# The SSD decay matrices move from the attention stage to the gate projections

## The chip, the cores and the metric

The kernel runs on one core of a Trainium2 chip. The metric is the device time of one execution in microseconds; several executions are taken and their median is given. In the profile PE is the matmul engine and PEld its weight load, DVE the vector engine, ACT the engine for activation functions, POOL the general one, and SP the engine whose queue issues every DMA of this kernel.

## The reference

Two layers run over 1024 latent and 256 context tokens of width 1024. Each layer normalizes its tokens, projects them once, and feeds three branches: a state-space scan in two directions (SSD), grouped-query attention, and a conformer branch. The outputs are concatenated and projected back. The part of the SSD that the change touches, for chunks of 128 tokens:

```python
seg = cum[:, :, :, None] - cum[:, :, None, :]
mask = jnp.tril(jnp.ones((l, l), dtype=bool))[None, None, :, :, None, None]
lmat = jnp.exp(jnp.where(mask, seg, -jnp.inf))
cb = jnp.einsum('bclgn,bcsgn->bclsg', Cc, Bc)
y_diag = jnp.einsum('bclsg,bclsgr,bcsgrp->bclgrp', cb, lmat, xdt)
...
u = ua * jax.nn.sigmoid(ub)
u = jax.nn.silu(layernorm(dwconv(u, conv_w, conv_b), ln_g, ln_b))
u = u @ pw_w + pw_b
return u * jax.nn.silu(gate)
```

The last four lines are the conformer branch. The product of `cb` and `lmat` is the masked decay matrix, called E here: for each chunk, direction and group of six heads one tile of 128 x 768 numbers.

## The kernel before, in words

Tokens come in ten tiles of 128 (eight latent, two context). Large products run as three fp32r matmuls, since each operand is split into a high and a low part: `mm3` (L210) issues high times high, low times high, high times low, all through `mm` (L193). Transposes go through `tr` (L196), activations through `act` (L199), vector operations through `ts` (L203, L205) and `stt` (L208), and the power of -1/2 through `rs_pow` (L269, L271 on POOL). The order of instructions on each engine comes from a scheduler that follows priorities: `at(us)` sets the priority of what follows, and lower goes first. It also follows the pools: a pool has a fixed number of buffers for each name, they are handed out in the order in which the program asks for them, and who asks later waits for who asked earlier. PSUM has four pools: `pm` with four buffers ("m"), `pt` with two ("t"), `pv_` with one ("v") and `px` with one ("x").

`phase_b` (L434) makes the projections. After q, k and v it runs 17 weight blocks, `block(i)` (L623), each due 26 us after the one before. `wblock` (L349) loads the block's weights, copies them to `wth` on ACT and takes `wtl`, the rest, by a subtraction on POOL (L359). Blocks 0 to 8 give the inputs of the SSD and the conformer branch; their convolutions run on DVE, `conv_x` writes B and C transposed to DRAM (`bT_d`, `cT_d`), and `cac` holds the four convolved tiles of the conformer branch. Blocks 9 to 16 give the gates: `gate` (L590) takes a tanh on ACT, a product on DVE and stores the result (`gz_d`, `gc_d`, `ga_d`).

Beside blocks 11 to 16 runs the conformer branch's end, `cm_tail` (L656). For each tile of tokens it transposes `cac` into a "t" buffer, takes the mean and variance on DVE, normalizes (`xn`, one buffer), transposes back into the "x" buffer, scales and shifts (`lv`, L205), takes a tanh and a product, and splits the result into `uh` (ACT) and `ul` (POOL, L689), with one buffer for each of the two. For a group of tiles, (0,4), (4,4) and (8,2), in layer 1 the first two, the pointwise GEMM follows: for each of four blocks of features twelve matmuls into the "v" buffer, an eviction that multiplies by the gate (`gcs`, loaded from `gc_d`), and a store to `yc_d`.

Attention comes next, and the SSD's scan runs beside it. `attn_prep` (L841) prepares keys and queries: `kprep` (L849) loads `k_t` (L856, one buffer) in three parts, splits it on ACT and DVE (L860) and transposes it through the "v" buffer. `attn` (L904) issues the score products (`k_a`, `q_a`), takes maxima on DVE (`a_sm`, L935), exponentials on ACT (`a_p`), sums on DVE and POOL (`a_ac`, L974) and the scaled output (`a_a`, L981). `ssd` (L710) takes the chunks 25 us apart. For each chunk it loads B and C, multiplies them into the "x" buffer, masks the product on DVE (`s_cm`, L772), and for each direction and group loads the cumulative log decays as a broadcast (`s_cb`, L785), subtracts on POOL (L788), applies a relu and an exponential on ACT, and multiplies by the masked product on POOL (L791).

Of the kernel before, what the change touches and what calls it, by code (L numbers as in the profile page):

```python
# [9 lines left out]
F32R = mybir.dt.float32r  # L10
# [150 lines left out]
def build(tc, a, out, depth=DEPTH, dump=None):  # L161
# [4 lines left out]
    def at(us):  # L166
        tc.cur_priority = int(us * 100)

    def pool(st, name, bufs=1, **k):
        return st.enter_context(tc.tile_pool(name=name, bufs=bufs, **k))  # L170
# [3 lines left out]
    def mk(p, shape, tag, dt=F32, bufs=None):  # L174
        uid[0] += 1
        k = {} if bufs is None else {"bufs": bufs}
        return p.tile(shape, dt, tag=tag, name=f"{tag}_{uid[0]}", **k)
# [8 lines left out]
    def dr(shape, name, dt=F32):  # L186
        t = dp.tile(shape, dt, tag=name, name=name)
        if dump is not None:
            dump[name] = t
        return t  # L190

    def mm(o, l, r, start, stop):
        P.matmul(o, l, r, start=start, stop=stop)  # L193
# [4 lines left out]
    def act(o, i, f, **k):  # L198
        S.activation(o, i, f, **k)  # L199
# [58 lines left out]
    bT_d = dr([2, 128, T], "bT_d")  # L258
    cT_d = dr([2, 128, T], "cT_d")
    cum_d = dr([NT * 24, 128], "cum_d")  # L260
    gz_d = dr([6, 128, T], "gz_d")
    ga_d = [dr([128, T], f"ga_d{j}") for j in range(6)]
    gc_d = [dr([128, T], f"gc_d{j}") for j in range(4)]
# [170 lines left out]
    def phase_b(l, nh, b0, pp):  # L434
# [122 lines left out]
        def conv_x(j, t0):  # L557
            xp = xps[j]
            at(t0)
            o = mk(xp_p, [128, 1282], "xcv", bufs=2)  # L560
            w = sw[:, 5 * j:5 * j + 5]
            ts(V, o, xp[:, 0:1282], w[:, 0:1], ALU.mult, sw[:, 50 + j:51 + j], ALU.add)
            for k in range(1, 5):
                at(t0 + 2 * k)
                stt(o, xp[:, k:k + 1282], w[:, k:k + 1], o, ALU.mult, ALU.add)
            at(t0 + 10)
            th = mk(up_p, [128, 1282], "th")
            act(th, o, AF.Tanh)
            stt(o, th, 1.0, o, ALU.add, ALU.mult)
            if j >= 6:  # L570
                d = bT_d[j - 6] if j < 8 else cT_d[j - 8]
                Y.dma_start(out=d[:, 0:1024], in_=o[:, 0:1024])
                Y.dma_start(out=d[:, 1024:1280], in_=o[:, 1026:1282])
            if j < 8:
                at(t0 + XLAG)
                sg = mk(gp, [128, NT, 128], "xsg")
                for ta in (0, 4, 8):
                    n = min(4, NT - ta)
                    ps = mk(*((pt, [128, 4, 128], "t") if ta == 4 else (px, [128, 4, 128], "x")))
                    for t in range(ta, ta + n):  # L580
                        c0 = t * 128 + (2 if t >= 8 else 0)
                        tr(ps[:, t - ta, :], o[:, c0:c0 + 128], idf)
                    act(sg[:, ta:ta + n, :], ps[:, 0:n, :], AF.Copy)
                if j < 6:
                    d = xt_d[:, :, 128 * j:128 * j + 128]
                else:
                    d = bt_d[:, :, 128 * (j - 6):128 * (j - 6) + 128]
                Y.dma_start(out=d.rearrange("t p f -> p t f"), in_=sg)
# [64 lines left out]
        for i in range(9, 14):  # L653
            block(i)

        def cm_tail(c0):  # L656
            at(c0 - 10)
            pwh, pwl = wblock(tlp, wt, a["pww"][l], "pw", 1)
            hc = mk(tlp, [128, 16], "hc")
            ts(V, hc[:, 0:8], colc[l][:, CO["lng"][0]:CO["lng"][0] + 8], 0.5, ALU.mult)  # L660
            groups = [(0, 4), (4, 4)] + ([] if last else [(8, 2)])
            for tb, tn in groups:
                uh = mk(tlp, [128, 4, 512], "uh", F32R)
                ul = mk(tlp, [128, 4, 512], "ul", F32R)
                for t in range(tb, tb + tn):
                    at(c0 + 4 * t)
                    c1 = t * 128 + (15 if t >= 8 else 0)
                    ps = mk(pt, [128, 4, 128], "t")
                    for j in range(4):
                        tr(ps[:, j, :], cac[j][:, c1:c1 + 128], idf)  # L670
                    bs = mk(tlp, [128, 12], "bs", bufs=2)
                    V.bn_stats(bs[:, 0:6], ps.rearrange("p j t -> p (j t)"))
                    V.bn_aggr(bs[:, 6:8], bs[:, 0:6])
                    rs_pow(bs[:, 9:10], bs[:, 7:8], 1.0, bs[:, 8:9], 1)
                    xn = mk(gp, [128, 512], "xn", bufs=1)
                    ts(V, xn, ps.rearrange("p j t -> p (j t)"), bs[:, 6:7], ALU.subtract, bs[:, 9:10], ALU.mult)
                    ps2 = mk(px, [128, 4, 128], "x")
                    for j in range(4):
                        tr(ps2[:, j, :], xn[:, 128 * j:128 * j + 128], idf)
                    th = mk(tlp, [128, 4, 128], "lth", bufs=1)  # L680
                    v2 = mk(tlp, [128, 4, 128], "lv2", bufs=1)
                    for j in range(4):
                        g, b = hc[:, j:j + 1], hc[:, 4 + j:5 + j]
                        ts(V, v2[:, j], ps2[:, j], g, ALU.mult, b, ALU.add)
                    act(th, v2, AF.Tanh)
                    stt(v2, th, 1.0, v2, ALU.add, ALU.mult)
                    o = (t - tb) * 128
                    act(uh[:, :, o:o + 128], v2, AF.Copy)
                    G.tensor_tensor(ul[:, :, o:o + 128], v2, uh[:, :, o:o + 128].bitcast(F32), ALU.subtract)  # L689
                n = tn * 128  # L690
                at(c0 + 4 * (tb + tn))
                for f in range(4):
                    gcs = mk(gp, [128, 512], "gcs")
                    Y.dma_start(out=gcs[:, 0:n], in_=gc_d[f][:, tb * 128:tb * 128 + n])
                    ps = mk(pv_, [128, 512], "v")
                    pwx, ux = (pwh, pwl), (uh, ul)
                    mm3(ps[:, 0:n], lambda x, k: pwx[x][:, k, 128 * f:128 * f + 128],
                        lambda x, k: ux[x][:, k, 0:n], 4)
                    stt(gcs[:, 0:n], ps[:, 0:n], cc(l, "pwb", f), gcs[:, 0:n], ALU.add, ALU.mult)
                    ts(V, gcs[:, 0:n], gcs[:, 0:n], 0.5, ALU.mult)  # L700
                    Y.dma_start(out=yc_d[f][:, tb * 128:tb * 128 + n], in_=gcs[:, 0:n])
# [8 lines left out]
    def ssd(l, sp, c0, sv):  # L710
# [15 lines left out]
        def bc(x, n=NH, w=HD):  # L726
            return x.unsqueeze(2).to_broadcast([128, n, w])
# [27 lines left out]
        for c in [8, 9] + list(range(8)):  # L755
# [1 line left out]
            t0 += SSD_PACE  # L757
            xt, bt = load(c)
            if c < 8 or not last:
                bT = mk(sp, [128, 2, 128], "s_bT", bufs=2)  # L760
                cT = mk(sp, [128, 2, 128], "s_cT", bufs=2)
                tk = slice(128 * c, 128 * c + 128)
                Y.dma_start(out=bT, in_=bT_d[:, :, tk].rearrange("g p t -> p g t"))
                Y.dma_start(out=cT, in_=cT_d[:, :, tk].rearrange("g p t -> p g t"))
                gz = mk(sp, [128, 6, 128], "s_gz", bufs=1)
                Y.dma_start(out=gz, in_=gz_d[:, :, tk].rearrange("g p t -> p g t"))
                ps = mk(px, [128, 512], "x")
                for g in range(2):
                    mm(ps[:, 128 * g:128 * g + 128], bT[:, g, :], cT[:, g, :], True, True)
                cm = mk(sp, [128, 2, 2, 128], "s_cm", bufs=1)  # L770
                for d, m in enumerate((um, lm)):
                    V.tensor_tensor(cm[:, d], ps[:, 0:256].rearrange("p (g t) -> p g t", g=2),  # L772
                                    m.unsqueeze(1).to_broadcast([128, 2, 128]), ALU.mult)
                xd = []
                for d in range(2):
                    t = mk(sp, [128, 768], f"s_xd{d}", bufs=1)
# [2 lines left out]
                E = {}  # L779
                for g in range(2):  # L780
                    for d in range(2):
                        h0 = 12 * d + 6 * g
                        cb = mk(sp, [128, 6, 128], "s_cb", bufs=2)
                        src = cum_d[24 * c + h0:24 * c + h0 + 6, :].rearrange("h t -> (h t)")
                        Y.dma_start(out=cb.rearrange("p h t -> p (h t)"),  # L785
                                    in_=src.unsqueeze(0).to_broadcast([128, 768]))
                        e = mk(sp, [128, 6, 128], "s_e", bufs=4)
                        G.tensor_tensor(e, cb, bc(cum[:, c, h0:h0 + 6], 6, 128), ALU.subtract)  # L788
                        act(e, e, AF.Relu, scale=-1.0)
                        act(e, e, AF.Exp, scale=-1.0)  # L790
                        G.tensor_tensor(e, e, cm[:, d, g].unsqueeze(1).to_broadcast([128, 6, 128]), ALU.mult)  # L791
                        E[d, g] = e
                yo = mk(sp, [128, 768], "s_yo", bufs=1)
                G.tensor_tensor(hv(yo), hv(xt), bc(rc(l, "d")), ALU.mult)
# [412 lines left out]
```

## Time and profile before

| | |
|---|---|
| runs, us | 2926.68, 2923.34, 2924.92 |
| median, us | 2924.92 |
| profiled execution, us | 2925.86 |
| its span, us | 2924.0 |
| mean granted PE clock | 0.976 of full |
| DMA traffic | 314.44 MB, 108 GB/s over the span |

The span runs from the first to the last instruction that the profiler shows; the profiled execution's own time is 1.9 us longer. Busy time counts an engine from the start to the end of its instructions; matmuls overlap, so their mean duration is longer than the distance from one start to the next. The stages follow each other within each layer: the gate projections of layer 0 lie at 534 to 799 us and its attention at 806 to 1360, those of layer 1 at 2017 to 2226 and 2236 to 2730. In a row of a group the count stands behind an x, then the busy time in us and the mean duration of one in ns, then the engine's idle time before them and what ended it.

### The profile page before, as it was taken

To read this page: it belongs to the slowest core of one execution; us is meant where nothing else is said; L and a number is where in the kernel's file an instruction comes from. 1 tells how busy PE (TensorE), PEld (TensorE's weight loads), DVE (VectorE), ACT (ScalarE), POOL (GpSimd) and SP (SyncE) were. 2 spreads that over 40 slices of the span, in tenths; PEclk is the share of its full clock that TensorE was granted. 3 is DMA by queue.
4 is the path that set the end of the run, shared out by engine and by line. 5 is a ranking of instruction groups with operands and counts; after the bars stand their busy time and mean duration, and the time that the engine had idled before them with its cause. 6 is when DMAs were issued, how large, how long until landed. Compare 5 with 4: busy or idle time off the path is not lost. (4 is left out here: it accounts for less than half of the span.)

```text
span 2924.0 us, 41060 instructions
## 1 busy us (share of the span) xinstructions
PE 2775.7 (95%) x15708; PEld 2058.5 (70%) x15708; DVE 2167.2 (74%) x2987; ACT 1068.0 (37%) x1801; POOL 1167.3 (40%) x832
## 2 busy tenths in 40 slices
PE   5999998999999999899999999999998999999998
PEld 3888876888855555565787998877886565555676
DVE  4576899973288889887545577999834889898744
ACT  4212221222245555454335322222223455644532
POOL 2244122232166767662112353122322676775111
PEclk8999998999999999999999999999999999999999
DMA  6541111223342323223745322113335232321654
GB/s 237 191 160 66 56 55 62 92 92 112 101 144 84 102 68 104 67 76 99 213 153 161 122 77 68 56 55 98 111 118 168 74 98 77 95 64 43 185 154 144
DMA packets 284035, 314.44 MB, mean 108 GB/s; under 512 B 27606, under 2 KB 219190, under 8 KB 282814
## 3 DMA queue, kind: packets, MB, share of 16 engines
q1 hardware_dynamic: 283838, 311.82, 33.5%
q8 instruction: 123, 2.02, 0.3%
q14 instruction: 74, 0.61, 0.1%
HBM read 236.25 MB, written 75.50 MB: 107 GB/s over the span
## 5 line engine op out<-in xcount | busy, mean ns | idle before, releaser
L193 PE MATMUL m<-hh,wth 128*128 128x512 f32 (+1 forms) x1440 | 534.9, 371 | 0.1
L193 PE MATMUL m<-hl,wth 128*128 128x512 f32 (+1 forms) x1440 | 533.4, 370 | 0.0
L193 PE MATMUL m<-hh,wtl 128*128 128x512 f32 (+1 forms) x1440 | 532.7, 370 | 0.0
L199 ACT ACTIVATE a_p<-m 128x512 f32<-128x512 f32 x492 | 289.0, 595 | 374.0 <-PE m L193 370.6
L208 DVE SCALAR_TENSOR_TENSOR cac<-up,cmw,cac 128x1295 f32<-128x1295 f32 (+1 forms) x240 | 385.4, 1627 | 2.0
L935 DVE TENSOR_REDUCE a_sm<-m 128x1 f32<-128x512 f32 (+1 forms) x600 | 332.5, 582 | 46.9 <-PE m L193 45.0
L359 POOL TENSOR_TENSOR wtl<-wr,wth 128x1024 fp32r<-128x1024 f32 x68 | 200.3, 2945 | 406.6 <-ACT wth L199 406.6
L193 PE MATMUL t<-a_p,vs 128*64 128x256 f32 x1968 | 324.0, 405 | 0.7 <-DVE a_rc L1010 0.3
L193 PEld LDWEIGHTS m<-hh,wth 128*128 128x128 f32 x1440 | 274.0, 190 | 48.0 <-ACT th L199 0.5
L193 PEld LDWEIGHTS m<-hh,wtl 128*128 128x128 f32 x1440 | 273.5, 190 | 48.3
L193 PEld LDWEIGHTS m<-hl,wth 128*128 128x128 f32 x1440 | 273.8, 190 | 47.4
L193 PE MATMUL m<-q_a,k_a 128*128 128x512 f32 (+1 forms) x656 | 259.7, 406 | 6.1 <-DVE a_sm L935 4.6
L193 PE MATMUL m<-k_a,q_a 128*128 128x512 f32 (+1 forms) x600 | 247.0, 437 | 13.6 <-DVE a_sm L935 9.8
L193 PE MATMUL m<-woh,yh 128*128 128x512 f32 x576 | 225.8, 395 | 8.2 <-issue 3.3
L193 PE MATMUL m<-woh,yl 128*128 128x512 f32 x576 | 228.8, 398 | 4.4 <-DVE yl L1099 4.3
L193 PE MATMUL m<-wol,yh 128*128 128x512 f32 x576 | 226.5, 394 | 0.0
L193 PE MATMUL m<-q_b,k_b 65*128 65x512 f32 (+1 forms) x656 | 218.8, 344 | 0.0
L193 PEld LDWEIGHTS m<-q_a,k_a 128*128 128x128 f32 x656 | 125.9, 192 | 107.1 <-issue 52.0
L193 PEld LDWEIGHTS t<-a_p,vs 128*64 128x64 f32 x1968 | 104.3, 136 | 133.9 <-issue 95.3
L193 PEld LDWEIGHTS m<-k_a,q_a 128*128 128x128 f32 x600 | 113.5, 195 | 113.3 <-issue 45.2
L199 ACT ACTIVATE wth<-wr 128x1024 fp32r<-128x1024 f32 (+1 forms) x84 | 89.3, 1064 | 256.3 <-DMA wr<-in_wfm 134.5
L193 PE MATMUL m<-wth,hh 128*128 128x256 f32 (+1 forms) x608 | 173.7, 288 | 0.6 <-DVE c_qn L474 0.5
(239 smaller groups left out, 5604.4 us busy)
## 6 DMA issues: line engine op xcount, KB each, us to landing
wr<-in_wfm SPq DMA_DIRECT2D x68, 512.0 KB, 3.6
s_cb<-cum_d SPq DMA_DIRECT2D x72, 384.0 KB, 3.7
ada_w<-in_adaw SPq DMA_DIRECT2D x32, 512.0 KB, 4.2
wor<-in_wout SPq DMA_DIRECT2D x64, 256.0 KB, 3.1
s_x<-xt_d SPq DMA_DIRECT2D x38, 384.0 KB, 3.0
yf<-ys_d SPq DMA_DIRECT2D x36, 384.0 KB, 4.0
yf<-ya_d SPq DMA_DIRECT2D x36, 384.0 KB, 4.2
yf<-yc_d SPq DMA_DIRECT2D x36, 256.0 KB, 2.9
```

The lines of the kernel that those rows point to most:

```text
L193: P.matmul(o, l, r, start=start, stop=stop)
L199: S.activation(o, i, f, **k)
L208: V.scalar_tensor_tensor(o, i, s, i1, op0, op1)
L359: (e or G).tensor_tensor(lo[:, s], raw, hi[:, s].bitcast(F32), ALU.subtract)
L935: V.tensor_reduce(sm[:, 2 * x + t, j:j + 1], ps[:, 0:kn], axis=AX.X, op=ALU.max)
```

## The change

A new function, `decays`, makes the four matrices E of a chunk and stores them to a new DRAM tensor, one for each chunk. It is called for all chunks behind `block(13)` and ahead of `cm_tail` in the program, 18 us apart from 8 us after block 9's due time. In `ssd` the code that made E is gone, and four loads stand in its place. To make room, the conformer tail works on pairs of tiles, five in layer 0 and four in layer 1: `uh`, `ul` and `gcs` are half as wide, `gcs` has two buffers, and a helper tile, `xsg`, moves to another pool. In `decays`, the product of B and C uses the "x" buffer, e_b, e_c and the masked product e_m have one buffer each, and E (`e_e`) has three.

```diff
+    e_d = [dr([4, 128, 768], f"e_d{c}") for c in range(NT)]
...
-                sg = mk(gp, [128, NT, 128], "xsg")
+                sg = mk(xp_p, [128, NT, 128], "xsg")
...
         for i in range(9, 14):
             block(i)
+        def decays(c, t0):
+            cum = sv[1]
+            tk = slice(128 * c, 128 * c + 128)
+            at(t0)
+            bT = mk(ep, [128, 2, 128], "e_b")
+            cT = mk(ep, [128, 2, 128], "e_c")
+            Y.dma_start(out=bT, in_=bT_d[:, :, tk].rearrange("g p t -> p g t"))
+            Y.dma_start(out=cT, in_=cT_d[:, :, tk].rearrange("g p t -> p g t"))
+            at(t0 + 2)
+            ps = mk(px, [128, 512], "x")
+            for g in range(2):
+                mm(ps[:, 128 * g:128 * g + 128], bT[:, g, :], cT[:, g, :], True, True)
+            cm = mk(ep, [128, 2, 2, 128], "e_m")
+            for d, m in enumerate((um, lm)):
+                V.tensor_tensor(cm[:, d], ps[:, 0:256].rearrange("p (g t) -> p g t", g=2),
+                                m.unsqueeze(1).to_broadcast([128, 2, 128]), ALU.mult)
+            for d in range(2):
+                for g in range(2):
+                    h0 = 12 * d + 6 * g
+                    at(t0 + 4 * (2 * d + g))
+                    e = mk(ep, [128, 6, 128], "e_e", bufs=3)
+                    src = cum_d[24 * c + h0:24 * c + h0 + 6, :].rearrange("h t -> (h t)")
+                    Y.dma_start(out=e.rearrange("p h t -> p (h t)"), in_=src.unsqueeze(0).to_broadcast([128, 768]))
+                    G.tensor_tensor(e, e, bc(cum[:, c, h0:h0 + 6], 6, 128), ALU.subtract)
+                    act(e, e, AF.Relu, scale=-1.0)
+                    act(e, e, AF.Exp, scale=-1.0)
+                    G.tensor_tensor(e, e, cm[:, d, g].unsqueeze(1).to_broadcast([128, 6, 128]), ALU.mult)
+                    Y.dma_start(out=e_d[c][2 * d + g], in_=e.rearrange("p h t -> p (h t)"))
+
+        ep = pool(s3, f"ep{l}")
+        for i, c in enumerate(range(8) if last else [8, 9] + list(range(8))):
+            decays(c, g0 + 8 + 18 * i)
...
-            groups = [(0, 4), (4, 4)] + ([] if last else [(8, 2)])
+            groups = [(b, 2) for b in range(0, 8 if last else NT, 2)]
             for tb, tn in groups:
-                uh = mk(tlp, [128, 4, 512], "uh", F32R)
-                ul = mk(tlp, [128, 4, 512], "ul", F32R)
+                uh = mk(tlp, [128, 4, 256], "uh", F32R)
+                ul = mk(tlp, [128, 4, 256], "ul", F32R)
...
-                    gcs = mk(gp, [128, 512], "gcs")
+                    gcs = mk(gp, [128, 256], "gcs", bufs=2)
...
-                bT = mk(sp, [128, 2, 128], "s_bT", bufs=2)
-                Y.dma_start(out=bT, in_=bT_d[:, :, tk].rearrange("g p t -> p g t"))
-                ps = mk(px, [128, 512], "x")
-                for g in range(2):
-                    mm(ps[:, 128 * g:128 * g + 128], bT[:, g, :], cT[:, g, :], True, True)
-                cm = mk(sp, [128, 2, 2, 128], "s_cm", bufs=1)
...
                         e = mk(sp, [128, 6, 128], "s_e", bufs=4)
-                        G.tensor_tensor(e, cb, bc(cum[:, c, h0:h0 + 6], 6, 128), ALU.subtract)
-                        act(e, e, AF.Relu, scale=-1.0)
-                        act(e, e, AF.Exp, scale=-1.0)
-                        G.tensor_tensor(e, e, cm[:, d, g].unsqueeze(1).to_broadcast([128, 6, 128]), ALU.mult)
+                        Y.dma_start(out=e.rearrange("p h t -> p (h t)"), in_=e_d[c][2 * d + g])
```

The order of the instructions follows from the scheduler, so the places that matter are shown from it. On PE of the kernel before, late in the gate projections of layer 0 (m is a projection's PSUM buffer, v the pointwise GEMM's):

```order
L193 MATMUL m_6421<-hh_153,wth_6321 128x512
L193 MATMUL m_6421<-hl_154,wth_6321 128x512
L193 MATMUL m_6421<-hh_153,wtl_6322 128x512
L193 MATMUL v_6097<-uh_6003,pwh_5627 128x256
L193 MATMUL v_6097<-ul_6004,pwh_5627 128x256
L193 MATMUL v_6097<-uh_6003,pwl_5628 128x256
...
L193 MATMUL m_6421<-hh_153,wth_6321 128x512
L193 MATMUL m_6421<-hl_154,wth_6321 128x512
```

The last pair's pointwise products stand between products of one projection. On PE after the change, the end of the last projection of layer 0:

```order
L193 MATMUL m_7212<-hh_163,wth_7052 128x256
L193 MATMUL m_7212<-hl_164,wth_7052 128x256
L193 MATMUL m_7212<-hh_163,wtl_7053 128x256
L196 MATMUL t_6317<-msk_74,cac_429_2758 128x128
L196 MATMUL t_6317<-msk_74,cac_430_2759 128x128
L196 MATMUL t_6317<-msk_74,cac_431_2760 128x128
L196 MATMUL t_6317<-msk_74,cac_432_2761 128x128
L193 MATMUL v_6090<-ul_6033,pwh_6020 128x256
L193 MATMUL v_6090<-uh_6032,pwl_6021 128x256
...
L193 MATMUL v_6656<-uh_6544,pwl_6021 128x256
L196 MATMUL v_7259<-idr_76,k_h_7255 128x128 x4
```

The pointwise GEMM of the first pair begins at the last projection, and those of the four other pairs follow it in rows that hold no projection, up to the first transposes of `kprep`. The first transposes of a normalized tile stand 90 rows ahead of the last projection's end in layer 0, with 77 projection matmuls behind them; all twenty products of B and C of the stage stand ahead of them. In layer 1 it is 18 projection matmuls.

On POOL, in the same stage, before the change:

```order
L359 TENSOR_TENSOR wtl_6322<-wr_6323,wth_6321 128x1024
L271 TENSOR_TENSOR bs_6037<-bs_6037,neg_82 128x1
L689 TENSOR_TENSOR ul_5822<-lv_767_5922,uh_5821 128x4x128
L359 TENSOR_TENSOR wtl_6322<-wr_6327,wth_6321 128x1024
L689 TENSOR_TENSOR ul_6004<-lv_783_6023,uh_6003 128x4x128
L359 TENSOR_TENSOR wtl_6512<-wr_6513,wth_6511 128x1024
L689 TENSOR_TENSOR ul_6004<-lv_789_6050,uh_6003 128x4x128
```

and after it, where the first pair's `ul` is made:

```order
L684 TENSOR_TENSOR e_e_6006<-e_e_6006,d_cum_1695 128x768
L727 TENSOR_TENSOR ul_6033<-lv_795_6052,uh_6032 128x4x128
L687 TENSOR_TENSOR e_e_6006<-e_e_6006,e_m_5989 128x768
L684 TENSOR_TENSOR e_e_6013<-e_e_6013,d_cum_1695 128x768
L272 TENSOR_TENSOR bs_6194<-bs_6194,neg_82 128x1
L687 TENSOR_TENSOR e_e_6013<-e_e_6013,e_m_5989 128x768
L727 TENSOR_TENSOR ul_6033<-lv_801_6079,uh_6032 128x4x128
```

The first pair's `ul` stands among the last matrices E of the stage (subtraction L684, multiplication L687); before, each `ul` (L689 there, L727 here) stood between two weight splits.

More of the change, by code (lines that the diff above doesn't have):

```diff
@@ L654, in phase_b, with bc @@
             block(i)
+        def bc(x, n, w):
+            return x.unsqueeze(2).to_broadcast([128, n, w])
+        def decays(c, t0):
[29 more added lines that the diff above has]
+            decays(c, g0 + 8 + 18 * i)
         def cm_tail(c0):
@@ L766, in ssd @@
                 Y.dma_start(out=gz, in_=gz_d[:, :, tk].rearrange("g p t -> p g t"))
-                ps = mk(px, [128, 512], "x")
-                for g in range(2):
-                    mm(ps[:, 128 * g:128 * g + 128], bT[:, g, :], cT[:, g, :], True, True)
-                cm = mk(sp, [128, 2, 2, 128], "s_cm", bufs=1)
-                for d, m in enumerate((um, lm)):
-                    V.tensor_tensor(cm[:, d], ps[:, 0:256].rearrange("p (g t) -> p g t", g=2),
-                                    m.unsqueeze(1).to_broadcast([128, 2, 128]), ALU.mult)
                 xd = []
@@ L781, in ssd @@
                     for d in range(2):
[L782 to L786, printed above, removed]
                         e = mk(sp, [128, 6, 128], "s_e", bufs=4)
-                        G.tensor_tensor(e, cb, bc(cum[:, c, h0:h0 + 6], 6, 128), ALU.subtract)
-                        act(e, e, AF.Relu, scale=-1.0)
-                        act(e, e, AF.Exp, scale=-1.0)
-                        G.tensor_tensor(e, e, cm[:, d, g].unsqueeze(1).to_broadcast([128, 6, 128]), ALU.mult)
+                        Y.dma_start(out=e.rearrange("p h t -> p (h t)"), in_=e_d[c][2 * d + g])
                         E[d, g] = e
```

## The prediction

> **What bounds the kernel now.** I read the page of the profile first, then the windows of the stages that the change touches, then the timeline where those stages meet, then what TensorE (PE) waits for.
>
> ```profile
> span 2924.0 us, 41060 instructions
> PE 2775.7 (95%) x15708; PEld 2058.5 (70%) x15708; DVE 2167.2 (74%) x2987; ACT 1068.0 (37%) x1801; POOL 1167.3 (40%) x832
> ```
>
> The profiled run took 2925.86 us, 1.9 more than its span and 0.9 more than the median of 2924.92. PE is busy for 95% of the span, so an edit pays only where PE waits, and it costs where it makes PE wait. The windows are the gate projections and the attention of layer 0, then of layer 1; the columns are width, then busy time of PE, PEld, DVE, ACT and POOL, then granted clock, DMA share and GB/s.
>
> ```profile
> 534.00:799.00 265.00, 262.66 (x1380) 223.40 (x1379) 145.37 (x203) 59.74 (x93) 64.39 (x36) 0.99 0.30 102
> 806.00:1360.00 554.00, 525.74 (x3261) 309.98 (x3262) 479.33 (x683) 284.16 (x481) 365.66 (x221) 0.96 0.29 87
> 2017.00:2226.00 209.00, 207.76 (x931) 168.75 (x931) 123.92 (x158) 49.79 (x71) 56.98 (x32) 1.00 0.34 114
> 2236.00:2730.00 494.00, 483.10 (x2972) 279.13 (x2972) 439.77 (x624) 258.18 (x441) 321.34 (x187) 0.99 0.29 89
> ```
>
> In the gate stages PE has no idle time worth the name (2.3 and 1.2 us) while POOL is free for three quarters. In attention PE idles 28.3 and 10.9 us, 39 together; DVE is busy for 87 and 89% of those windows and POOL for two thirds. What PE waits for there, in layer 0 and in layer 1 (sum, times, longest):
>
> ```profile
> PE t L193 <- DVE a_a L981: 12.3, 7, 3.6
> PE m L193 <- DVE a_sm L935: 6.9, 8, 2.2
> ```
> ```profile
> PE m L193 <- DVE a_sm L935: 7.5, 10, 1.5
> PE t L193 <- DVE a_a L981: 0.7, 2, 0.4
> ```
>
> So 27.4 of the 39 us are waits for DVE. The seam between the stages is short now. In each pair of rows stand the last projection and the first score matmul:
>
> ```profile
> 799.23 0.28 PE L193 MATMUL m<-hh,wtl 128*128 128x256 f32 x1
> 806.69 0.80 PE L193 MATMUL m<-k_a,q_a 128*128 128x512 f32 x1 [0.99 <-ACT q_a L199]
> ```
> ```profile
> 2226.43 0.39 PE L193 MATMUL m<-hh,wtl 128*128 128x512 f32 x1
> 2236.32 1.20 PE L193 MATMUL m<-k_a,q_a 128*128 128x512 f32 x1
> ```
>
> That is 7.5 us in layer 0 and 9.9 in layer 1, because the conformer tail (its transposes, its pointwise GEMM) lies among the projections, behind which its long chain costs nothing.
>
> **The decay matrices leave attention.** Eighteen chunks, four matrices each:
>
> ```profile
> L788 POOL TENSOR_TENSOR s_e<-s_cb,d_cum 128x768 f32<-128x768 f32 x72 | 117.8, 1646 | 55.0 <-PE x L193 51.6 <-DMA s_cb<-cum_d 3.3
> L791 POOL TENSOR_TENSOR s_e<-s_e,s_cm 128x768 f32<-128x768 f32 x72 | 152.3, 2145 | 24.6 <-DVE s_cm L772 23.6 <-ACT q_b L199 1.0
> L199 ACT ACTIVATE s_e<-s_e 128x768 f32<-128x768 f32 x144 | 118.9, 840 | 21.7 <-POOL s_e L788 20.1
> L193 PE MATMUL x<-s_cT,s_bT 128*128 128x128 f32 x72 | 12.2, 293 | 0.0
> s_cb<-cum_d SPq DMA_DIRECT2D x72, 384.0 KB, 3.7
> ```
>
> POOL loses 270 of its 687 us there, ACT 119 of 542, PE 12. The 72 broadcast loads become 72 loads of the finished matrix of the same 384 KB, with four buffers to fetch ahead, so SP's queue carries no more; the loads of B go. Nothing of this is PE's bound. What it can return is PE's idle time. POOL is not what PE waits for; it sits behind DVE. I take the DVE waits above as the gain, 26 of 27.4 (a_a and a_sm come early when the sums and the softmax chain are not behind POOL or ACT). The ends are 0 (DVE's own work is nearly the same, 919 us) and 39 (all of PE's idle time).
>
> **The gate stage takes them.** Added there, per chunk: four subtractions, four multiplications on POOL (15.2 us), eight ACT passes (6.7), two small products on PE, two masks on DVE, four broadcast loads, four 384 KB stores. In layer 0 by the order POOL has 38 subtractions, 37 multiplications and 12 weight splits ahead of the first tile's tail.
>
> ```profile
> L359 POOL TENSOR_TENSOR wtl<-wr,wth x13: 2384/2407/3406, 548.4 to 745.6; 128x1024 fp32r<-128x1024 f32 x13
> ```
>
> 38 x 1.646 + 37 x 2.145 + 12 x 2.41 = 171 us. PE gets to the first B.C product 203 rows after block 9's start at 534, near 573, and to the first tile's transposes near 755 (77 projections of some 0.2 us before 771, below): 182 us. POOL is full but just fits; I add 8 us per layer for its lag (0 if DVE and POOL don't collide; 40 if each op takes a quarter longer). In layer 1 it is 31 x 1.646 + 30 x 2.145 + 12 x 2.41 = 144 us in some 141. DMA share rises by 56 MB in 474 us, 118 GB/s over 102 to 114: hidden, since the share is 0.30 to 0.34.
>
> **The tail moves behind the projections.** This carries the forecast. The normalized tile's transposes and the B.C products share one PSUM buffer, handed out in the order of the program, and the program now asks for all B.C products first. So in PE's order only 77 projections (layer 0) and 18 (layer 1) are left behind the first tile's transposes, and every pointwise matmul but a few stands behind the last projection. Widths and spacings, pointwise (12 of 256 columns, first and last) and projection (512):
>
> ```profile
> 764.13 0.28 PE L193 MATMUL v<-uh,pwh 128*128 128x256 f32 x1
> ...
> 765.43 0.28 PE L193 MATMUL v<-uh,pwl 128*128 128x256 f32 x1
> ```
> ```profile
> 785.17 0.39 PE L193 MATMUL m<-hl,wth 128*128 128x512 f32 x1
> 785.40 0.40 PE L193 MATMUL m<-hh,wtl 128*128 128x512 f32 x1
> ```
>
> 0.118 us per 256 columns and 0.23 per 512. PE's own pointwise time hardly changes: layer 0 96 x 0.23 + 48 x 0.118 = 27.7 before, 240 x 0.118 = 28.3 now; layer 1 22.1 and 22.7. It only moves, so the projections end earlier: 799 - 28 = 771 (the transposes that leave and the B.C products that come in are some 6 us each), and 2227 - 22 = 2205 less 1 in layer 1. Now the chain of one tile, which now runs in the open:
>
> ```profile
> 698.56 1.36 DVE L205 TENSOR_SCALAR lv<-x,hc 128x128 f32<-128x128 f32 x4
> 700.02 0.63 ACT L199 ACTIVATE lth<-lv 128x512 f32<-128x512 f32 x1 [2.20 <-DVE lv L205]
> 700.68 0.69 DVE L208 SCALAR_TENSOR_TENSOR lv<-lth,lv 128x512 f32<-128x512 f32 x1
> 701.41 0.64 ACT L199 ACTIVATE uh<-lv 128x512 fp32r<-128x512 f32 x1 [0.76 <-DVE lv L208]
> 702.12 1.29 POOL L689 TENSOR_TENSOR ul<-lv,uh 128x512 fp32r<-128x512 f32 x1
> ...
> 705.20 1.05 DVE L205 TENSOR_SCALAR lv<-x,hc 128x128 f32<-128x128 f32 x3 [0.75 <-PE x L196]
> ```
>
> From one tile's scaling to the next tile's it is 6.6 us. With one buffer each for uh and ul, a pair's second tile can't start until the pair before has gone through its GEMM. That GEMM:
>
> ```profile
> 765.75 0.48 DVE L208 SCALAR_TENSOR_TENSOR gcs<-v,colc,gcs 128x256 f32<-128x256 f32 x1 [3.12 <-PE v L193]
> ```
> ```profile
> gcs<-gc_d SPq DMA_DIRECT2D x4, 128.0 KB, 2.0
> yc_d<-gcs SPq DMA_DIRECT2D x4, 128.0 KB, 1.7
> ```
> ```profile
> 485.00:490.00 5.00, 0.00 (x0) 0.00 (x0) 5.00 (x5) 0.00 (x0) 0.20 (x3) 0.50 0.33 88
> ```
>
> Where PE idles the granted clock is 0.50, so twelve matmuls take 1.4 to 2.8 us; with the eviction 0.48 and a gap each, two feature blocks take 5.2, and the third and fourth wait until a gcs buffer has been stored and loaded again (1.7 + 2.0). I take 10 us a pair (7.6 at full clock and with gcs in time, 14 with SP's queue behind). A pair in the open is 6.6 + 10 = 16.6.
>
> Behind it stands kprep, whose transposes use the same PSUM buffer and whose SBUF space is the tail's. Before, its loads were issued as the GEMM ended, with projections over them; now nothing lies over them.
>
> ```profile
> 766.20 0.70 SPq L856 DMA_DIRECT2D k_t<-k_d  x1
> ...
> 772.96 0.63 ACT L199 ACTIVATE k_h<-k_t 128x512 fp32r<-128x512 f32 x1 [1.43 <-DMA k_t<-k_d]
> ...
> 774.13 0.37 SPq L856 DMA_DIRECT2D k_t<-k_d  x1
> ```
> ```profile
> 800.46 0.38 SPq L856 DMA_DIRECT2D k_t<-k_d  x1
> ```
>
> The third load came 6.2 us ahead of the first score matmul. Two rounds before it take 3.9 each as an estimate (the row's 7.9 with v and q in the queue is the upper end): 14.
>
> Layer 0: 771 + 10 (first pair) + 4 x 16.6 + 14 + 8 lag = 869, against 806.7: +62. Layer 1: the first tile at 2200, two chains 13, then 10 + 3 x 16.6 + 14 + 8 = 2295, against 2236.3: +59.
>
> By the Trainium skill, page "SBUF — State Buffer", section "SBUF: two separate sides", DVE and GpSimd share one port pair as an exclusive lock, and the loser blocks for the whole instruction.
>
> ```profile
> L208 DVE SCALAR_TENSOR_TENSOR lv<-lth,lv x18: 674/1222/2480, 618.7 to 2164.2; 128x512 f32<-128x512 f32 x18
> ```
>
> One shape on DVE takes 0.67 to 2.48 us here, which agrees. By that rule the move takes 270 us of lock away from attention's DVE, which PE waits for, and puts it on the gate stages', which have room; attention then gives back all 39 us, the third rival's 3007.
>
> **The sum.** 2925.9 + 62 + 59 - 26 = 3021; against the median 0.9 less: 3020.
>
> **The rivals.**
> 1. *POOL becomes the bound of the gate stage.* For it: 171 of 182 us and 144 of 141 leave no slack, and POOL also holds the weight split that the next projection needs and ul of each tile. If its operations take a quarter longer, 43 and 36 us come on top, less the 16 assumed: about 3083. Against: POOL's medians were taken in attention, where DVE was busier than here.
> 2. *Attention gives nothing back.* DVE's 919 us there stay, and its share is already 87%: 3046.
> 3. *Attention gives back all its idle time*, since DVE's operations get shorter when POOL's are gone (the spread of 0.67 to 2.48 us for one shape speaks for it, an idle time that isn't DVE's to end, 12 of 39 us, against): 3007.
> 4. *The tail is short.* A pair takes about 11 us, as the chains of the next tile overlap the GEMM and gcs comes in time: 7 pairs x 5.6 = 39 less, 2981.
> 5. *Faster.* The same overlap goes further: with the one buffer of uh no limit, a tile costs only the PSUM buffer's cycle (4 transposes 0.6, scaling 1.36, about 2.5 us), a pair 8, no POOL lag: layer 0 771 + 10 + 32 + 14 = 827, +20; layer 1 2200 + 5 + 10 + 24 + 14 = 2253, +17; with all 39 given back 2924, and below it if kprep too is quicker. It decides at 8 us a pair. Against it stands the chain of rows above, 6.6 us, of which at most one tile per pair can be prepared ahead.
> That the change doesn't do what it says is excluded by the order: E is loaded, not made, in attention.
>
> **How the numbers follow.** Main case 0.50 (3020), POOL bound 0.16, nothing back 0.12, all back 0.10, short tail 0.07, faster or level 0.05. The range has to reach from short tail to POOL bound: 2965 to 3100, leaving out the faster case and a POOL bound worse than a third. About 0.2% (6 us) is what a measurement of this kernel tells from no change. Faster 0.04, same 0.02, slower 0.94.
>
> **What would show it.** Right: a stretch of 90 to 110 us in layer 0 and 85 to 100 in layer 1 between the last projection and the first score matmul in which PE is busy for less than half at a granted clock near 0.5, waiting for uh, ul, lv and gcs; POOL at 85% or more in the gate stages; attention stages 10 to 15 us shorter each. Wrong: that stretch below 50 us, projections that wait for weight splits (POOL the bound), or attention windows of the old length.

## The result, and the profile after

The changed kernel takes 3095.08 us, the median of four runs (3087.96 to 3102.39), against 2924.43 for the kernel before. The ratio is 1.0583, with a 95% interval of 1.0557 to 1.0608: slower by 5.8%, some 171 us. The forecast was slower by 95 us, with a range up to 3100; the time lies 5 us inside that end.

The profiled run took 3096.16 us. The page's first lines:

```profile
span 3094.4 us, 42053 instructions
PE 2830.3 (91%) x15900; PEld 2106.1 (68%) x15900; DVE 2114.6 (68%) x3019; ACT 1071.6 (35%) x1801; POOL 1140.1 (37%) x832
```

PE falls from 95% to 91% of a longer span; its work is 55 us more, in part because matmuls at a lower clock last longer (a pointwise one takes 0.42 us at 843.0 to 846.4 us, where the granted clock is 0.50, and 0.28 at 846.8 to 852.0, where it is 1.00). The windows after the change, with the columns of before: the decays' part of layer 0's gate stage, the stretch between the last projection and the first score product, attention; then the last two for layer 1.

```profile
584.00:805.00 221.00, 201.47 (x1016) 170.76 (x1017) 78.92 (x102) 96.04 (x135) 176.91 (x98) 0.95 0.65 218
806.00:914.00 108.00, 62.73 (x318) 50.66 (x316) 48.20 (x115) 19.24 (x33) 20.28 (x20) 0.70 0.37 119
914.00:1454.00 540.00, 520.38 (x3258) 305.02 (x3258) 445.30 (x683) 236.31 (x425) 207.46 (x138) 0.97 0.30 91
...
2318.00:2422.00 104.00, 57.08 (x274) 46.13 (x273) 43.86 (x103) 21.74 (x35) 26.88 (x22) 0.66 0.39 127
2422.00:2902.00 480.00, 472.40 (x2927) 273.58 (x2926) 408.10 (x616) 217.64 (x389) 187.73 (x120) 0.99 0.29 88
```

In the stretches every engine is busy for less than two thirds and the granted clock is 0.70 and 0.66: a chain runs there, and nobody's throughput bounds it. To see where the 170 us of span lie, the first and last start of four groups on PE are enough: the feature-major projections (m<-hh,wtl), the pointwise GEMM (v<-uh,pwl), the score products (k_a,q_a) and their low part (q_b,k_b). In the rows, duration in ns as least, median and largest, then first and last start. Before, layer 0 and layer 1:

```profile
L193 PE MATMUL m<-hh,wtl x816: 274/392/628, 242.1 to 799.2; 128*128 128x512 f32 x109, 128*128 128x256 f32 x55
L193 PE MATMUL m<-q_b,k_b x336: 277/390/628, 824.9 to 1368.9; 65*128 65x512 f32 x84, 65*128 65x256 f32 x84
...
L193 PE MATMUL m<-hh,wtl x624: 274/392/632, 1762.7 to 2226.4; 128*128 128x512 f32 x136, 128*128 128x256 f32 x20
L193 PE MATMUL m<-q_b,k_b x320: 278/340/628, 2252.8 to 2728.8; 65*128 65x512 f32 x80, 65*128 65x256 f32 x80
```

And after:

```profile
L193 PE MATMUL m<-hh,wtl x816: 274/392/628, 248.5 to 805.5; 128*128 128x512 f32 x109, 128*128 128x256 f32 x55
L193 PE MATMUL v<-uh,pwl x80: 276/280/420, 806.5 to 889.8; 128*128 128x256 f32 x80
L193 PE MATMUL m<-k_a,q_a x312: 274/397/796, 913.9 to 1436.2; 128*128 128x512 f32 x96, 128*128 128x256 f32 x60
L193 PE MATMUL m<-q_b,k_b x336: 278/389/628, 930.6 to 1454.4; 65*128 65x512 f32 x84, 65*128 65x256 f32 x84
...
L193 PE MATMUL m<-hh,wtl x624: 274/392/775, 1849.2 to 2318.1; 128*128 128x512 f32 x136, 128*128 128x256 f32 x20
L193 PE MATMUL v<-uh,pwl x64: 276/352/420, 2332.8 to 2398.6; 128*128 128x256 f32 x64
L193 PE MATMUL m<-k_a,q_a x288: 277/399/1049, 2422.7 to 2878.1; 128*128 128x512 f32 x96, 128*128 128x256 f32 x48
L193 PE MATMUL m<-q_b,k_b x320: 278/388/442, 2439.2 to 2902.1; 65*128 65x512 f32 x80, 65*128 65x256 f32 x80
```

| stretch | before, us | after, us | difference |
|---|---|---|---|
| start to first feature-major projection | 242.1 | 248.5 | +6.4 |
| to the last projection, layer 0 | 557.1 | 557.0 | 0 |
| to the first score product | 7.5 | 108.4 | +100.9 |
| attention, to the last q_b | 562.2 | 540.5 | -21.7 |
| to layer 1's first feature-major projection | 393.8 | 394.8 | +1.0 |
| to the last projection, layer 1 | 463.7 | 468.9 | +5.2 |
| to the first score product | 9.9 | 104.6 | +94.7 |
| attention, to the last q_b | 492.5 | 479.4 | -13.1 |
| to the end of the span | 195.2 | 192.3 | -2.9 |

The two seams are more than the whole loss; attention gives some of it back. What PE waits for in the first (806 to 914 us) are the links of the conformer tail and of kprep:

```profile
PE x L196 <- DVE lv L205: 10.6, 3, 3.6
PE v L196 <- ACT k_h L199: 8.1, 2, 7.7
PE v L193 <- ACT uh L199: 7.9, 2, 5.7
PE v L193 <- DVE gcs L208: 7.7, 10, 1.5
PE v L193 <- POOL ul L727: 3.0, 4, 0.8
```

And in the gate stage (541 to 806 us), where before PE had one wait of 2.3 us:

```profile
PE x L193 <- issue: 14.8, 6, 4.9
PE x L193 <- DVE cac L208: 3.7, 1, 3.7
PE t L196 <- DVE cac L208: 3.0, 1, 3.0
```

The first row is PE in front of the products of B and C. The profile names no releaser for them ("issue"), so the rows around one such wait have to tell it:

```profile
703.60 3.56 POOL L687 TENSOR_TENSOR e_e<-e_e,e_m 128x768 f32<-128x768 f32 x2
...
707.19 0.75 DVE L675 TENSOR_TENSOR e_m<-x,msk 128x256 f32<-128x256 f32 x2 [3.83 <-POOL e_e L687]
708.05 1.19 PE L193 MATMUL x<-e_c,e_b 128*128 128x128 f32 x4 [4.87 <-issue]
```

DVE's masks wait for the last multiplication of the chunk before (one e_m buffer), the next product waits for the masks (one x buffer), and PE takes its instructions in order, so the projections behind it wait too: here PE stood still for 4.87 us.

### The profile page after: what moved, and what is told of

It is laid out like the page before. It is cut to its first block, busy times and chain, and to the rows that moved or that the text cites. A ratio compares the mean times of both kernels' runs of the same rounds, so it can differ in the third digit from the quotient of the medians.

```text
span 3094.4 us, 42053 instructions
## 1 busy us (share of the span) xinstructions
PE 2830.3 (91%) x15900; PEld 2106.1 (68%) x15900; DVE 2114.6 (68%) x3019; ACT 1071.6 (35%) x1801; POOL 1140.1 (37%) x832
## 5 line engine op out<-in xcount | busy, mean ns | idle before, releaser
L208 DVE SCALAR_TENSOR_TENSOR cac<-up,cmw,cac 128x1295 f32<-128x1295 f32 (+1 forms) x240 | 406.8, 1716 | 1.9
L208 DVE SCALAR_TENSOR_TENSOR g_o<-g_t,m 128x512 f32<-128x512 f32 (+1 forms) x80 | 50.3, 630 | 223.5 <-ACT g_t L199 217.4
```

The source lines that it names most:

```text
L208: V.scalar_tensor_tensor(o, i, s, i1, op0, op1)
```

## The experiments

Three questions were open. Is it the order in the x buffer that exposes the tail (theory A)? Do the pairs cost anything by themselves (rival B)? And what sets the pace of the decays, 22 us a chunk (584 to 805 us for ten) where 18 were planned: POOL's work (rival C) or the cycle of the three E buffers (theory E)? Ratios are against the kernel before on the same chip.

**Pairs alone.** The kernel before, with

```diff
-                sg = mk(gp, [128, NT, 128], "xsg")
+                sg = mk(xp_p, [128, NT, 128], "xsg")
...
-            groups = [(0, 4), (4, 4)] + ([] if last else [(8, 2)])
+            groups = [(b, 2) for b in range(0, 8 if last else NT, 2)]
...
-                uh = mk(tlp, [128, 4, 512], "uh", F32R)
-                ul = mk(tlp, [128, 4, 512], "ul", F32R)
+                uh = mk(tlp, [128, 4, 256], "uh", F32R)
+                ul = mk(tlp, [128, 4, 256], "ul", F32R)
...
-                    gcs = mk(gp, [128, 512], "gcs")
+                    gcs = mk(gp, [128, 256], "gcs", bufs=2)
```

> The kernel before with one part of the change alone: the conformer tail in pairs of tiles, with half-wide uh, ul and gcs. The decay matrices stay in attention. Theory A (the tail is exposed because its transposes stand behind the B.C products in the one x buffer): pairs cost next to nothing while they lie among the projections, 2920 to 2945 us. Rival B (the pairs themselves, with more and smaller groups, make the tail long): 3000 us or more. Rival C (POOL's load in the gate stage is the bound): as A.

Measured: 2982.01 us, ratio 1.0179 (1.0162 to 1.0196). Both were off: the pairs with the moved xsg aren't free, and don't cost what B says. The last pointwise product of layer 0 (765.4 us before, and the projections ended at 799.2):

```profile
L193 PE MATMUL v<-uh,pwl x80: 277/279/281, 652.0 to 803.6; 128*128 128x256 f32 x80
```

It ends with the projections (805.3 here), so kprep's chain stands bare behind it, and the first score product comes 24 us after the last projection in place of 7.5 (26 for 9.9 in layer 1). That is a cost of the pairs which needs no wait for the x buffer; the forecast had put the exposed tail and kprep down to that buffer alone.

**Pairs with two buffers for uh and ul**, the SBUF of before: `"uh", F32R, bufs=2` and `"ul", F32R, bufs=2`.

> As pairs_only (xsg moved), with two buffers for uh and for ul, which is the SBUF space of before. Theory A for the pairs' cost (with one buffer a pair's second tile waits for the GEMM of the pair before, 31 us a pair, so that the last GEMM ends with the last projection and kprep stands bare behind it): the last pointwise product comes 25 to 40 us earlier and the stretch falls from 24 and 26 us to about 10: 2945 to 2958 us. Rival (the rounds of loads and stores of gcs or the priorities set the pace of a pair): 2975 to 2986 us.

Measured: 2943.68 us, ratio 1.0061 (1.0041 to 1.0081), 1 us below the expected range.

```profile
L193 PE MATMUL v<-uh,pwl x80: 276/280/282, 650.8 to 785.4; 128*128 128x256 f32 x80
```

The GEMM ends 18 us earlier (25 to 40 were expected), and the stretch is 9.8 us and 11.7 in layer 1. So the single buffer, which makes a pair's second half wait for the GEMM of the pair before, is what made most of the pairs' price here; the narrow GEMMs did not. No run has the changed kernel with two such buffers.

**Pairs with xsg where it was** (`mk(gp, ...)` again).

> As pairs_only, but the helper tile xsg stays in the pool where it was before. In pairs_only the first feature-major projection starts 5.9 us later than before and the stretch between the layers' output products and the next layer's first such projection is 12 us longer, both far from the conformer tail. Theory D (the move of xsg shifts the buffers of the right-hand pools onto space that earlier work still uses): both go away, 2960 to 2970 us. Rival (they come with the pairs' other order of instructions): 2978 to 2986 us.

Measured: 2960.88 us (1.0111; 1.0083 to 1.0140). The time agrees with theory D. The trace agrees in part: the first feature-major projection is 5.1 us earlier than in pairs_only (242.8 for 247.9), but the stretch between the layers (from the first output product of layer 0 to layer 1's first such projection) lost 2 of the 12 us only.

**Both together**, the test of what is left:

> The kernel before with the conformer tail in pairs, two buffers for uh and ul, and xsg where it was before. It parts what is left of the pairs' cost (pairs_two_uh, about 14 us): if the move of xsg is the rest (theory D), 2925 to 2937 us; if smaller GEMMs and more rounds of gcs are, 2937 to 2948 us.

Measured: 2932.09 us (1.0013; 1.0000 to 1.0026), as theory D had it. Pairs with two buffers and xsg in its place cost nothing that stands out. By the ratios of these two pairs of runs, moving xsg costs 20 us with one buffer for uh and 14 with two; with two the stretch between the layers lost 9 us. That buffers of other pools come to lie on space that earlier work still uses was not shown. (The kernel with attention's side alone, below, starts its first feature-major projection at 247.5 us with xsg in its place, but four stores more stand in SP's queue there, and its loads behind them start 3.8 us later, so it says nothing on this.) The cause of that part stays open.

**Decays of one chunk alone.** The changed kernel, in which chunk 0's decays are made and every scan loads them; those of the other chunks are left out.

```diff
-        for i, c in enumerate(range(8) if last else [8, 9] + list(range(8))):
+        for i, c in enumerate([0]):
...
-                        Y.dma_start(out=e.rearrange("p h t -> p (h t)"), in_=e_d[c][2 * d + g])
+                        Y.dma_start(out=e.rearrange("p h t -> p (h t)"), in_=e_d[0][2 * d + g])
```

> The changed kernel with the decay matrices of one chunk alone made in the gate stage; every chunk's scan loads those of that chunk, so nine of ten chunks' decays are left out. Attention's loads stay as they are. Theory A: the pointwise products go back among the projections, the stretch between last projection and first score product is 10 to 30 us, attention keeps what it gave back (22 + 13 us): 2880 to 2920 us. Rival B (pairs): the stretch stays near 100 us, 3040 us or more. Rival C (POOL): as A, since POOL's load is gone too.

Measured: 2965.83 us (1.0124; 1.0105 to 1.0144). Above theory A's range, which did not have the pairs' cost yet; with the 51 us of pairs_only the range would be 2931 to 2971.

```profile
L193 PE MATMUL v<-uh,pwl x80: 277/279/281, 662.1 to 813.8; 128*128 128x256 f32 x80
```

The GEMM is back among the projections (which end at 815.4), and the stretch is 21 us, as with the pairs alone. Against pairs_only, attention is 17 us shorter in layer 0 and 23 in layer 1.

**The x buffer in turn.** All the work of the changed kernel, with the program asking for the buffer by due time:

```diff
-        for i, c in enumerate(range(8) if last else [8, 9] + list(range(8))):
-            decays(c, g0 + 8 + 18 * i)
+        due = [(8 + 18 * i, 0, c) for i, c in enumerate(range(8) if last else [8, 9] + list(range(8)))]
...
-                    at(c0 + 4 * t)
+                    yield
+                    at(c0 + 13 * t)
...
-        cm_tail(g0 + TAIL)
+        tail = cm_tail(g0 + TAIL)
+        next(tail)
+        due += [(TAIL + 13 * t, 1, t) for t in range(8 if last else NT)]
+        for t0, k, c in sorted(due):
+            if k:
+                next(tail, None)
+            else:
+                decays(c, g0 + t0)
```

`cm_tail` stops at `yield` before each tile, and its due times follow at 13 us a tile in place of 4.

> The changed kernel with all its work, but the program asks for the x buffer in turn: one chunk's decays, then one tile of the conformer tail, in order of due times (chunk i at 8 + 18 i, tile t at 40 + 13 t us). Theory A: most of the pointwise products stand among the projections again, the stretch behind them shrinks from 108 and 105 us to 30 to 60: 2930 to 3000 us. Rival C (POOL's load bounds the gate stage): POOL does the same work in the same stage, 3060 us or more.

Measured: 3032.46 us (1.0357; 1.0325 to 1.0390): between theory A's range and rival C's.

```profile
L193 PE MATMUL v<-uh,pwl x80: 277/279/419, 670.5 to 854.3; 128*128 128x256 f32 x80
```

The GEMM starts 136 us earlier than in the changed kernel, and the stretch behind the last projection (849.0) falls from 108 us to 29, in layer 1 from 105 to 55. That is the order in the x buffer, shown: the edit's other part, the tiles' due times, makes them later and not earlier. But the projections themselves take 43 and 22 us longer. Most of the GEMM stands among them again (216 of its 240 matmuls in layer 0, 144 of 192 in layer 1), as it did in the kernel before, and PE's waits there are 31 us in layer 0, where the change had 22 and the kernel before 2: PE meets the chain's links among the projections, in order. So the kernel is still 3.6% slower than before.

**Three half-size mask buffers**, so that the masks wait less for POOL:

```diff
-            cm = mk(ep, [128, 2, 2, 128], "e_m")
+            cm = [mk(ep, [128, 2, 128], "e_m", bufs=3) for d in range(2)]
```

> The changed kernel with one edit: the masked product has three half-size buffers in place of one full one, so that a chunk's masks, and with them the x buffer, wait less for POOL's last multiplication of the chunk before. Theory A with its second part (PE's 15 and 8 us of waits at the B.C products come from this buffer): these waits go and the tail starts 10 to 25 us earlier in each layer, 3045 to 3080 us. Rival C (POOL's load sets the pace of the decays): 3085 to 3100 us, as the POOL work is the same.

Measured: 3091.41 us (1.0548; 1.0530 to 1.0566, where the change has 1.0557 to 1.0608). A miss for theory A's second part, and inside rival C's range; the next two runs decide between C and E. The waits at the products fall from 14.8 to 9.1 us, but the tile's transposes wait 8.1 for the masks. The wait moves along the chain, and the chain isn't faster.

**POOL's multiplication left out** (E lacks the masked product):

> The changed kernel without POOL's multiplication by the masked product (72 x 1.85 us of POOL's work left out; loads, subtraction, ACT and stores stay). Rival C (POOL's work sets the pace of the decays, 22 us a chunk): the chunk falls to about 15 us, the tail starts 40 to 60 us earlier in each layer and goes partly back under projections: 2980 to 3040 us. Theory E (the cycle of load, POOL, ACT, store through three buffers sets it): the cycle loses 1.85 of some 13 us, 3060 to 3085 us.

Measured: 3067.97 us, ratio 1.0473 (1.0443 to 1.0502). **The stores left out**, but for chunk 0's, which every scan loads:

```diff
-                    Y.dma_start(out=e_d[c][2 * d + g], in_=e.rearrange("p h t -> p (h t)"))
+                    if c == 0:
+                        Y.dma_start(out=e_d[c][2 * d + g], in_=e.rearrange("p h t -> p (h t)"))
```

> The changed kernel with the stores of E left out but for those of chunk 0, which every chunk's scan then loads. POOL's and ACT's work is all there. Theory E (the buffers' cycle, of which the store's 3.8 us is a part): chunks come 4 to 6 us closer, the tail starts 25 to 45 us earlier, 3020 to 3070 us. Rival C (POOL's work): 3085 to 3100 us.

Measured: 3049.32 us, ratio 1.0410 (1.0388 to 1.0432). Both fall into theory E's ranges and out of rival C's. The decays' multiplications of layer 0 on POOL, in the changed kernel and then without the stores:

```profile
L687 POOL TENSOR_TENSOR e_e<-e_e,e_m x40: 1801/1848/3160, 591.3 to 803.2; 128x768 f32<-128x768 f32 x40
```
```profile
L687 POOL TENSOR_TENSOR e_e<-e_e,e_m x40: 1815/1854/3150, 594.5 to 777.0; 128x768 f32<-128x768 f32 x40
```

With the same POOL work but 3.7 us less in each buffer's cycle, ten chunks end 26 us earlier. From the first row to the last that is 18.7 us a chunk in place of 21.7, and POOL is busy for 93% of 584 to 779 us, where the change keeps it busy for 80% of 584 to 805. So POOL had room that the change didn't use: its work is a link of the cycle, but not the bound. SP's queue shows the cycle itself in the changed kernel (584 to 805 us; L683 is the load of an E buffer, L688 the store):

```profile
SPq L683 <- DMA e_d<-e_e: 64.8, 31, 5.7
SPq L688 <- POOL e_e L687: 36.9, 31, 3.3
```

Of 40 loads 31 waited until the store of an earlier matrix had landed. The cycle's links alone (3.9 us to load, 1.47 for the subtraction, twice 0.85 on ACT, 1.85 for the multiplication, 3.7 to store) are 12.6 us, which with three buffers is 16.8 a chunk; the rest of the 21.7 are waits between the links. Whether loads were also late because they stand in the same queue behind stores that wait for POOL (the second row) no run parts, and a fourth buffer for E, the direct test, was not tried.

Without the multiplication the last store is issued 34 us earlier (at 770.8 for 805.0), 18.1 us a chunk from the first store to the last. But the first score product, counted from the first feature-major projection, comes only 13 us earlier in layer 0 (19.5 without the stores), since the projections then stall more (the last one is at 814.7); in layer 1 the two runs are level (30.5 and 29.4 us earlier). Both runs come down to about the 18 us a chunk that the program plans, so neither need say how fast such a cycle could go.

**Attention's side alone.** The kernel before, in which each scan loads its four tiles from DRAM, where a constant stands in for E; the making of E is left out everywhere.

> The kernel before with attention's side of the change alone: each chunk loads its four tiles from DRAM, where a constant stands in for E; the making of E is left out everywhere, the tail is as before. This is the most that the move could bring. Theory A (attention is worth what the two stages gave back, 27 us, and some of the 8 us at their ends): 2885 to 2905 us. Rival F (attention gave back only what the later start had cost it): 2915 to 2930 us.

Measured: 2883.08 us, ratio 0.9853 (0.9834 to 0.9872): 43 us are the most that the move could bring. They come in attention: it takes 536.0 and 476.0 us, from the first score product to the last q_b, where it took 562.2 and 492.5. Why it brings them is in DVE's rows; the running sum of attention before, after the change, and here:

```profile
L974 DVE TENSOR_TENSOR a_ac<-a_ac,a_p 128x1024 f32<-128x1024 f32 x72 | 118.6, 1647 | 12.7 <-ACT a_p L199 12.0
```
```profile
L995 DVE TENSOR_TENSOR a_ac<-a_ac,a_p 128x1024 f32<-128x1024 f32 x72 | 96.1, 1335 | 18.2 <-ACT a_p L199 17.7
```
```profile
L960 DVE TENSOR_TENSOR a_ac<-a_ac,a_p 128x1024 f32<-128x1024 f32 x72 | 101.8, 1413 | 18.0 <-ACT a_p L199 17.4
```

The same instruction takes 1.65 us on the mean beside POOL's decays and 1.34 to 1.41 without them. The trace of the kernel before also parts the 72 sums one by one: the 24 during which POOL ran no operation took 1.22 us on the mean (1.16 to 1.23), the 48 others 1.86 (1.21 to 2.80). The shape that the prediction showed with 0.67 to 2.48 us, `lv`, parts the same way: 0.67 to 0.69 us in the eight without POOL, 2.03 on the mean in the ten others. The maxima `a_sm` (128 x 512, read from PSUM) take 0.68 us either way.

**A subtraction for ACT.** If POOL stretches DVE, half of the gain might be had without moving anything: the kernel before, with

```diff
-                        G.tensor_tensor(e, cb, bc(cum[:, c, h0:h0 + 6], 6, 128), ALU.subtract)
-                        act(e, e, AF.Relu, scale=-1.0)
+                        for h in range(6):
+                            act(e[:, h], cb[:, h], AF.Relu, scale=-1.0, bias=cum[:, c, h0 + h:h0 + h + 1])
```

> The kernel before, with POOL's subtraction and the relu replaced by six relu instructions on ACT for each matrix, which take the difference as a per-partition bias; everything else stays. POOL loses 118 us of attention, ACT gains six passes of 128 in place of one of 768, some 1.9 us more a matrix as an estimate from the 0.45 us of such passes in the norms. Theory G (POOL's operations stretch DVE's, on which PE waits): 2905 to 2922 us. Rival H (ACT's added 134 us delay the exponentials that DVE and PE wait for): 2930 to 2950 us.

Measured: 2982.41 us (1.0201; 1.0179 to 1.0223), beyond both ranges. ACT's two rows for E:

```profile
L199 ACT ACTIVATE s_e<-s_cb,d_cum 128x128 f32<-128x128 f32 x432 | 132.5, 390 | 36.1 <-PE x L193 20.9 <-DMA s_x<-xt_d 7.8 <-issue 6.4
L199 ACT ACTIVATE s_e<-s_e 128x768 f32<-128x768 f32 x72 | 59.2, 839 | 0.1
```

ACT gained 73 us (192 for 119), less than expected, and the time grew by 56. Theory G holds as to DVE, whose running sum falls to 1.55 us on the mean, but it's no use here. The trace speaks for rival H, with a larger price than it had: DVE's sums (L974) waited 35.7 us for the exponentials (15.3 before). And PE was busy 45 us longer in the two attention stages with nearly the same matmuls, at a granted clock of 0.94 and 0.95 where it had been 0.96 and 0.99. That the exponentials stand behind the 24 small passes of each chunk was not tried by itself.

## Why the prediction was right, and where its terms were off

- **What bounds the kernel**: right. PE's idle time is what moved, and the loss lies at the seams.
- **The tail moves behind the projections** (forecast's main case): right in mechanism. From the last projection to the last pointwise product it was to take 84 us in layer 0 (10 + 4 x 16.6 + 8) and 77 in layer 1; it took 84.3 and 80.5. That layer 0 fits so closely is luck. The last products of the first, the second and the fifth pair:

```profile
816.57 0.28 PE L193 MATMUL v<-uh,pwl 128*128 128x256 f32 x1
...
834.83 0.28 PE L193 MATMUL v<-uh,pwl 128*128 128x256 f32 x1
...
889.85 0.41 PE L193 MATMUL v<-uh,pwl 128*128 128x256 f32 x1
```

  The first pair ends 11 us behind the last projection and each of the four others takes 18.3, not 16.6; the 8 us for POOL's lag don't appear in this stretch, for the first pair's GEMM had begun by the last projection. The two errors cancel. The interleaved kernel showed the x buffer as cause, and the pairs alone showed that the change has a second one, the single buffer of uh.
- **The projections end earlier by 28 and 23 us**: wrong, the largest miss. In layer 0 they end where they did before, in layer 1 5 us later. The GEMM's 28 us of PE left layer 0's stage, but PE waits 22 there, mostly for the B.C products and the convolution, and does the products, some 6. The step "POOL is full but just fits; 8 us for its lag" asked the wrong question, the sum of POOL's work, where the cycle of load, POOL, ACT, store through three buffers sets the pace (22 us a chunk), and PE, which takes the products in order among the projections, waits with it. The order's rows showed the products of B and C among the projections; that they could stall them was not priced.
- **kprep in the open, 14 us**: too small. 24.1 us in both layers:

```profile
890.74 0.66 SPq L877 DMA_DIRECT2D k_t<-k_d  x1
...
898.60 0.38 SPq L877 DMA_DIRECT2D k_t<-k_d  x1
...
903.49 0.37 SPq L877 DMA_DIRECT2D k_t<-k_d  x1
```

  The rounds took 7.9 and 4.9 us, and the first score product came 10.4 after the third load; the forecast's upper end for a round (7.9) was the better value for the first.
- **Attention gives back 26 us**: 21.7 and 13.1 in the windows, and 26.2 and 16.5 where the making of E is left out (free_matrices). That is 35 us, between the forecast's 26 and the third rival's 39; the second rival's nothing is refuted. The forecast's reason was good: PE's waits for a_a and a_sm in layer 0 fell from 12.3 and 6.9 us to

```profile
PE t L193 <- DVE a_a L1002: 7.6, 7, 1.8
PE m L193 <- DVE a_sm L956: 4.3, 6, 1.5
```

  but it's worth more than those waits, since DVE's operations themselves get shorter (1.86 us for a running sum that meets an operation of POOL, 1.22 for one that doesn't). That is the third rival's mechanism. By the Trainium skill, page "SBUF — State Buffer", section "SBUF: two separate sides", DVE and GpSimd share one port pair as an exclusive lock, whose loser blocks; the trace agrees with these two numbers.
- **Moving xsg**: not in the sum. Between kernels with pairs it costs 14 to 20 us. In the table above, the rows ahead of the two layers' projections, where it showed between those kernels, have only 6.4 and 1.0 us; how much of the change's time is its doing is not shown.
- **POOL as the bound** (rival 1, 3083): nearer the time than the main case, and wrong as to the cause. Its condition, that POOL's operations take a quarter longer, did not come (their means fell, 1.99 us for 2.15 and 1.61 for 1.65), POOL is at 80%, and without the stores, which POOL doesn't issue, the same POOL work is done 26 us sooner.
- **The signs that it named**: the stretch is 108 and 105 us (90 to 110 and 85 to 100 were named), with waits for uh, ul, lv and gcs as forecast. But PE is busy there for 58 and 55%, not for less than half, the clock is 0.70 and 0.66, not near 0.5, and POOL is at 80 and 77%, not 85. That the time lies inside the range is in part luck: it needed the room that was left for a POOL bound, which isn't what happened.

The misses add up: 28 + 28 for the projections, 20 for kprep, 7 ahead of the projections in the two layers, 4 for layer 1's tail, less 12 for attention and what follows it (37.7 for 26), is 75 us, which is the table's 170 less the forecast's 95.

## What to carry to other kernels

A pool with one buffer that is handed out in program order is a lock between two chains: whoever is written first runs first, however the priorities are set. Before work is moved into a stage whose busy engine takes its instructions in order, ask for each of its small instructions there what it waits for, and not only whether the other engines have time. And shrinking a buffer to make room is part of a change's price: here the pairs and the moved helper tile cost 52 us by themselves, where the whole change costs 171.

## What was not expected of the hardware

- Away from attention POOL's own operations get little shorter: the multiplication of 128 x 768 has a mean of 1.99 us in the gate stage against 2.15, the subtraction 1.61 against 1.65, and their medians hardly move (1.85 against 1.86, and 1.47 in both). DVE's sums in attention gain far more (1.65 to 1.34).
- In the exposed stretches the mean granted clock was 0.70 and 0.66, not the 0.50 of a stretch in which PE stands still. It goes back and forth: 0.50 at 843.0 to 846.4 us, 1.00 at 846.8 to 852.0.
